# Gathering a scan's partial-array products into four stretches of matmuls

## The chip, the cores and the metric

The kernel runs on one core of one Trainium2 chip. The metric is the device time of one execution in microseconds; for the kernel before it is 1631.19 us, the median of three runs (1631.13 to 1631.39). A core has a matmul engine (TensorE, PE), whose weight loads are shown apart (PEld), a vector engine (VectorE, DVE), an engine for activation functions (ScalarE, ACT), a general one (GpSimd, POOL), a queue for transfers (SyncE, SP), and 16 DMA engines. PE writes its results into banks of PSUM, and a bank must be read by another engine before it is written again.

## The reference, cut to what matters

The kernel computes one step of a decoder of two layers, for 1024 prompt tokens and 8 x 8 sample tokens (1088 columns in all): first a state-space layer (SSD), then a pooling layer. The change lies in the state-space layer's scan, which takes chunks of 128 tokens, for eight groups of four heads with 64 rows each:

```python
def ssd_scan(x, dt, A, B, C, h0):
    ...
    CB = jnp.einsum('bctgn,bcsgn->bctsg', C, B)
    xdt = x * dt[..., None]
    y_intra = jnp.einsum('bctsgr,bcsgrp->bctgrp', CB[..., None] * decay, xdt)
    decay_end = jnp.exp(acum[:, :, -1:] - acum)
    chunk_states = jnp.einsum('bctgn,bctgr,bctgrp->bcgrpn', B, decay_end, xdt)
    chunk_decay = jnp.exp(acum[:, :, -1])
    def step(h, inp):
        s, d = inp
        return d[..., None, None] * h + s, h
    h_final, h_prev = lax.scan(step, ...)
    y_inter = jnp.einsum('bctgn,bctgr,bcgrpn->bctgrp', C, jnp.exp(acum), h_prev)
    y = (y_intra + y_inter).reshape(b, L, H, P)
    return y, h_final.reshape(b, H, P, N)
```

Then y is gated with z, divided by its root mean square over a group's 256 rows, and multiplied by the output weights:

```python
    gated = (y * jax.nn.silu(z.astype(jnp.float32))).reshape(b, L, N_GROUPS, D_INNER // N_GROUPS)
    gated = gated * lax.rsqrt(jnp.mean(gated * gated, axis=-1, keepdims=True) + EPS)
    ...
    return gated.astype(h.dtype) @ w_out, new_conv, new_ssm
```

The sample tokens start from eight states h0 of their own. Each layer's input is shifted, scaled and gated by vectors that come from the conditioning (adaLN): `mod = sc @ ada_w[i] + ada_b[i]`. All is float32.

## The kernel before, in words

Tokens lie along the free axis, features on the 128 partitions. A weight matrix is split into a high and a low part, and every product of the projections is three matmuls of a 128 x 128 block with 360 or 364 tokens (`mm1`, L182 to L184). These use the whole array.

**Scans and fills.** `ssd_layer` runs eight scans, g = 0 to 7, one after the other. Each is a Python generator (`scan_group`); between its steps, `FILL[g]` says how many units of other work are put in from the generator `self.fill` (`beside`). A unit is 24 full matmuls, a third of a projection tile or a piece of the output projection. In scans 0 to 4 the units are the projections of the groups 1, 2, 3, 4 and 6 (`BESIDE`), in scans 5 to 7 the first parts of the output projection, whose inputs were stored to DRAM (`gyd`) and are loaded and split again (`gr` to `gh` and `gl`, L742, L743).

**One scan.** `front(c)` prepares chunk c: B·C (L545) and three transposes (L549) into a bank `tr`; on ACT the exponentials ea (L543), M (four relus L556, one exponential L557), the copy Bt (L566) and cd (L574); on DVE cb, M, xd and ea (L559 to L575). Chunks go in pairs. `states(c)` makes the pair's state sums S (L588, full array) and two additions of h on DVE (L593 for the first of all, L597), with a multiplication by the decay on POOL between (L596). `rows(c)` makes the pair's output y: for each chunk and head, M·xd (L609) and, where there is a state, ea·h (L613). These use 64 of the array's columns, two heads side by side in two column halves; DVE adds the result to y (L580). The sample tokens need Z (L628, 32 columns), zsc on DVE, and four pairs of products (L641 and L644, 64 columns), and their front uses `dup` (L437, 64 columns) for the transposes; `state_sample` updates the sample's states (L660 to L665).

**The tail of a scan** runs into the next one, as the generator `rest`. It gates y (L700 to L702), squares it, and sums the squares with ones in 32 columns (L708); ACT then loads its table (L301) and takes logarithm and exponential (L711, L309); the result goes to DRAM and comes back as a broadcast rs (L713, L716), DVE multiplies y by it (L720), and y is stored to `gyd`.

**adaLN.** The vectors of the second layer and the gates of both are 16 blocks. Each is 8 sums of 32 columns into a bank (L253: 16 records with four heads, `ada_block`), a copy mp on ACT (L258), and two small full matmuls that pick the tokens (L262). Fourteen of the blocks are put into the projections of `BESIDE`, after the second and third units of the tiles 1, 2 and 3 (`ada_plan`); two come late.

**What sets the order.** A scheduler gives each engine its order, once, when the kernel is built: program order is the priority, and an instruction goes ahead of another when what it needs is there earlier by the scheduler's own estimate. `high_priority`, `issue_after` and dependencies added by hand steer it. In the kernel before, the row products, dup, Z, the sums of adaLN and those of squares stand each where the program issues them, with projection matmuls between them where the scheduler found them ready.

Of the kernel before, what the change touches and what calls it, by code (L numbers as in the profile page):

```python
# [50 lines left out]
FILL = (((1,) * 10 + (2,),) * 4 + ((1,) * 9 + (4, 5),) + ((3, 2, 2, 2, 2, 2, 2, 2, 2, 2, 3),) * 2 + ((2, 2, 2, 1, 1, 1, 1, 1, 2, 2, 1),))  # L51
# [46 lines left out]
class Build:  # L98
# [81 lines left out]
    def mm1(self, ps, w, k, act, ch, first, last):  # L180
        nc, (hi, lo), (ah, al), (a, n) = self.nc, w, act, ch
        nc.tensor.matmul(ps[:, :n], hi[:, k, :], ah[:, a:a + n], start=first, stop=False)  # L182
        nc.tensor.matmul(ps[:, :n], hi[:, k, :], al[:, a:a + n], start=False, stop=False)  # L183
        nc.tensor.matmul(ps[:, :n], lo[:, k, :], ah[:, a:a + n], start=False, stop=last)  # L184
# [55 lines left out]
    def ada_block(self, src):  # L240

# [56 lines left out]

    def ln_set(self, mm=None):

        ins = self.nc.scalar.preload_act_table_set("natural_log_exp_and_others")  # L301
        if mm is None:
            self.tc.keep_in_program_order(ins)
        else:
            self.tc.add_manual_dep(ins.ins, mm.ins.name, mybir.DependencyInfo(mybir.DependencyClass.Sync, mybir.DependencyReason.DATA), reason="ln_set")
# [81 lines left out]
    def proj_group(self, G):  # L387

        for ii in range(4):
# [17 lines left out]
            ada = self.ada_do(self.ada_plan[G["g"], ii]) if (G["g"], ii) in self.ada_plan else iter(())  # L407
            for c in range(3):
# [3 lines left out]
                if c:  # L412
                    next(ada, None)
# [90 lines left out]
    def scan_group(self, g, T):  # L504
# [16 lines left out]
        h = [None]  # L521
# [12 lines left out]
        def front(c):  # L534
# [9 lines left out]
            pt = pp.tile([P, 512], F32, tag="tr", bufs=2, name=self.name("tr"))  # L544
            nc.tensor.matmul(pt[:L, 384:384 + L], B[:, tok], C[:, tok], start=True, stop=True)  # L545
            for i, t in enumerate((xs[0], xs[1], B)):
                o = pt[:, 128 * i:128 * i + 128]
                if c < 8:
                    nc.tensor.transpose(o, t[:, tok], self.ident)  # L549
                else:  # L550
                    self.dup(o, t[:, tok])
# [31 lines left out]
        def states(c, F):  # L583
# [5 lines left out]
            for i in range(2):  # L589
                cd, Si = F[i][5], S[:, 256 * i:256 * i + 256]  # L590
                hn = gp.tile([P, 4, 64], F32, tag="h", bufs=3, name=self.name("h"))
                if h[-1] is None:
                    nc.vector.tensor_copy(hn.rearrange("p r q -> p (r q)"), Si)  # L593
                else:
                    hd = gp.tile([P, 4, 64], F32, tag="hd", bufs=1, name=self.name("hd"))
                    nc.gpsimd.tensor_tensor(out=hd, in0=h[-1], in1=cd.unsqueeze(2).to_broadcast([P, 4, 64]), op=ALU.mult)  # L596
                    nc.vector.tensor_tensor(out=hn, in0=hd, in1=Si.rearrange("p (r q) -> p r q", r=4), op=ALU.add)  # L597
                h.append(hn)

        def rows(c, F):  # L600

            py = [pp.tile([P, 512], F32, tag="y", bufs=2, name=self.name("y")) for _ in range(2)]
            for i in range(2):
                tok, M, xdt, _, _, _, ct = F[i]
                hc, a = h[-3 + i], 128 * i
                for q in range(2):
                    for rr in range(2):
                        r, o = 2 * q + rr, slice(64 * rr, 64 * rr + 64)
                        nc.tensor.matmul(py[q][o, a:a + 128], xdt[:, r, :], M[:, r, :], start=True, stop=(hc is None))  # L609
                    if hc is not None:  # L610
                        for rr in range(2):
                            r, o = 2 * q + rr, slice(64 * rr, 64 * rr + 64)
                            nc.tensor.matmul(py[q][o, a:a + 128], hc[:, r, :], ct[:, r, :], start=False, stop=True)  # L613
            for q in range(2):
                evac_y(py[q], q, slice(128 * c, 128 * c + 256), 256)

        def sample_inter():

# [4 lines left out]
            nc.gpsimd.tensor_copy(mv[:, :, 1, 8:16], cv[:, :, 1, :])  # L623
            Z = pp.tile([P, 512], F32, tag="S", bufs=1, name=self.name("Z"))
# [5 lines left out]
            zsc = gp.tile([P, 4, 64], F32, tag="hd", bufs=1, name=self.name("zsc"))  # L630
# [4 lines left out]
        def back_sample(F, zsc):  # L635
            tok, M, xdt, xde, Bt, _, ea = F
            for q in range(2):
                py = pp.tile([P, 512], F32, tag="y", bufs=2, name=self.name("y"))
                for rr in range(2):
                    r, o = 2 * q + rr, slice(64 * rr, 64 * rr + 64)  # L640
                    nc.tensor.matmul(py[o, :64], xdt[:64, r, :], M[:64, r, :64], start=True, stop=False)  # L641
                for rr in range(2):
                    r, o = 2 * q + rr, slice(64 * rr, 64 * rr + 64)
                    nc.tensor.matmul(py[o, :64], zsc[:, r, :], self.kc[:, K_SEL64:K_SEL64 + 64], start=False, stop=True)  # L644
                evac_y(py, q, tok, 64)
# [46 lines left out]
        F, h = F[0], h[-1]  # L692
        nc.sync.dma_start(self.io["hpT"][g], h.rearrange("p r q -> p (r q)"))
        st = back_sample(F, zsc)
# [9 lines left out]
        state_sample(*st, 1)  # L704

        ps = self.pp.tile([P, 512], F32, tag="y", bufs=2, name=self.name("ms"))
        for j in range(4):
            mm = nc.tensor.matmul(ps[32 * j:32 * j + 32, :272], self.ones[:, :32], sq[0][:, 272 * j:272 * j + 272], start=True, stop=True, tile_position=(0, 32 * j))  # L708
        rs = sq[1][:, :272]
# [526 lines left out]
    def run(self):  # L1236
# [3 lines left out]
        places = [(g, ii) for g in BESIDE for ii in (1, 2, 3) if (g, ii) != (BESIDE[-1], 3)]  # L1240
# [5 lines left out]
        for g in BESIDE:  # L1246
            for ii in range(4):
                items.append((io["win"][6 * g + ii], 8))
                if (g, ii) in self.ada_plan:
# [557 lines left out]
```

## Time and profile before

| what | value |
|---|---|
| median of three runs | 1631.19 us (1631.13 to 1631.39) |
| the profiled execution's own time | 1633.98 us |
| its span, first to last instruction | 1632.2 us |
| mean granted clock of TensorE | 0.994 |
| the eight scans in the trace | about 359 to 1010 us |
| DVE, ACT, POOL busy over the span | 79%, 50%, 30% |
| DMA | 275.60 MB, 169 GB/s in the mean |

The page of the profile is of one execution; engines are named as above. A row of a group names the line, the engine, the operation, "out<-in" by the program's tile names, how often it ran, its busy time and mean ns, and the idle time of the engine just before it with what ended that. A row of the timeline has start, duration, engine, line, operation and shape, and in brackets a wait with its releaser. `128*64` is the part of the array a matmul uses, rows by columns; `128x256` is the size of its input. Ends of matmuls are modelled, so durations of PE rows overlap: the distance between starts is what a matmul took.

### The profile page before, as it was taken

What the parts mean: (1) busy time and instruction counts of PE and PEld (TensorE: products, weight loads), DVE (VectorE), ACT (ScalarE), POOL (GpSimd) and SP (SyncE); (2) the same over time, 40 slices, a digit from 0 to 9 for tenths busy, and PEclk for the clock granted to TensorE, in tenths of its full rate; (3) what the DMA queues carried; (4) which work ended last, traced back from release to release, by engine and by line L of the source; (5) the groups of instructions that cost most, each with busy time, mean ns of one, the idle gap of its engine ahead of it and who ended that gap; (6) DMA issues with size and microseconds to landing.
All of it is one profiled execution on the core that took longest, in us unless ns stands there. A gap on an engine that the chain in (4) does not pass through costs nothing.

```text
span 1632.2 us, 30956 instructions
## 1 busy us (share of the span) xinstructions
PE 1601.1 (98%) x12061; PEld 1524.7 (93%) x12061; DVE 1290.3 (79%) x2140; ACT 816.7 (50%) x1565; POOL 495.2 (30%) x527
## 2 busy tenths in 40 slices
PE   8999999999999999999999999999999999999997
PEld 6899999998899888988998899999999999999997
DVE  6875779777788888789887867988889867577876
ACT  6653334456776767575645536632322333333364
POOL 0233556511221202121212222366667640000241
PEclk9999999999999999999999999999999999999999
DMA  9422232264555554668898533043333369565783
GB/s 346 163 98 84 93 109 71 105 203 133 183 162 167 165 186 135 217 232 299 276 332 284 201 137 111 29 142 112 102 112 99 129 213 367 166 170 173 167 164 119
DMA packets 122306, 275.60 MB, mean 169 GB/s; under 512 B 18192, under 2 KB 59312, under 8 KB 122160
## 3 DMA queue, kind: packets, MB, share of 16 engines
q1 hardware_dynamic: 118128, 260.91, 46.8%
q0 software_dynamic: 4032, 12.72, 4.5%
q8 instruction: 95, 1.56, 0.4%
q14 instruction: 51, 0.42, 0.1%
HBM read 201.12 MB, written 70.23 MB: 166 GB/s over the span
## 4 chain that ended last, share of the span: by engine, by line
PE 82%; DVE 7%; DMA 5%; issue 3%; ACT 2%; POOL 1%; SPq 0%; DVEq 0%; ACTq 0%; POOLq 0%
PE st L982 11%; PE st L980 11%; PE st L981 11%; PE mm L182 10%; PE mm L184 10%; PE mm L183 10%; DMA acb<-acd 2%; PE op L1197 2%; PE op L1198 2%; PE op L1196 2%; PE y L609 2%; PE S L588 2%; PE y L613 2%; PE am L253 1%; PE tr L549 1%
## 5 line engine op out<-in xcount | busy, mean ns | idle before, releaser
L982 PE MATMUL st<-hh,w 128*128 128x272 f32 x832 | 240.8, 289 | 2.3 <-DVE w L176 2.3
L980 PE MATMUL st<-hh,w 128*128 128x272 f32 x832 | 240.2, 289 | 0.0
L981 PE MATMUL st<-hl,w 128*128 128x272 f32 x832 | 239.7, 288 | 0.0
L982 PE MATMUL st<-t,w 128*128 128x272 f32 x624 | 179.6, 288 | 0.0
L980 PE MATMUL st<-t,w 128*128 128x272 f32 x624 | 179.6, 288 | 0.0
L981 PE MATMUL st<-t,w 128*128 128x272 f32 x624 | 179.2, 287 | 0.0
L182 PE MATMUL mm<-hh,wh 128*128 128x364 f32 (+1 forms) x528 | 178.4, 338 | 0.1
L184 PE MATMUL mm<-hh,wl 128*128 128x364 f32 (+1 forms) x528 | 174.6, 331 | 0.0
L183 PE MATMUL mm<-hl,wh 128*128 128x364 f32 (+1 forms) x528 | 173.7, 329 | 0.0
L174 ACT ACTIVATE w<-wr 128x512 fp32r<-128x512 f32 x104 | 65.6, 631 | 190.4 <-PE st L982 156.8
L982 PEld LDWEIGHTS st<-hh,w 128*128 128x128 f32 x832 | 156.4, 188 | 3.4 <-DVE w L176 3.4
L980 PEld LDWEIGHTS st<-hh,w 128*128 128x128 f32 x832 | 156.7, 188 | 0.3 <-issue 0.3
L981 PEld LDWEIGHTS st<-hl,w 128*128 128x128 f32 x832 | 156.8, 188 | 0.0
L596 POOL TENSOR_TENSOR hd<-h,cd 128x256 f32<-128x256 f32 x56 | 47.1, 842 | 353.6 <-DVE h L597 195.4
L182 PE MATMUL mm<-gh,wh 128*128 128x364 f32 (+1 forms) x384 | 130.2, 340 | 2.1 <-ACT raw L419 2.1
L1197 PE MATMUL op<-b,w 128*128 128x272 f32 x448 | 129.0, 288 | 1.3 <-DVE b L1126 1.3
L1198 PE MATMUL op<-b,w 128*128 128x272 f32 x448 | 129.0, 288 | 0.7 <-DVE w L1170 0.7
L1196 PE MATMUL op<-b,w 128*128 128x272 f32 x448 | 129.6, 289 | 0.0
L184 PE MATMUL mm<-gh,wl 128*128 128x364 f32 (+1 forms) x384 | 127.1, 331 | 0.0
L183 PE MATMUL mm<-gl,wh 128*128 128x364 f32 (+1 forms) x384 | 126.7, 330 | 0.1
L980 PEld LDWEIGHTS st<-t,w 128*128 128x128 f32 x624 | 117.7, 189 | 0.0
L982 PEld LDWEIGHTS st<-t,w 128*128 128x128 f32 x624 | 117.3, 188 | 0.0
(293 smaller groups left out, 4613.7 us busy)
## 6 DMA issues: line engine op xcount, KB each, us to landing
wr<-win SPq DMA_DIRECT2D x48, 512.0 KB, 3.7
acb<-acd SPq DMA_DIRECT2D x64, 256.0 KB, 3.9
wr<-pin SPq DMA_DIRECT2D x32, 512.0 KB, 3.6
wr<-pout SPq DMA_DIRECT2D x28, 512.0 KB, 3.9
x<-x1d SPq DMA_DIRECT2D x24, 544.0 KB, 6.3
x1d<-x SPq DMA_DIRECT2D x22, 544.0 KB, 5.4
wr<-pout POOLq DMA_DIRECT2D x20, 512.0 KB, 5.5
x<-xT SPq DMA_DIRECT2D x16, 544.0 KB, 6.0
```

The costliest lines, as they stand in the source:

```text
L174: self.nc.scalar.activation(hi, src, AF.Copy)
L182: nc.tensor.matmul(ps[:, :n], hi[:, k, :], ah[:, a:a + n], start=first, stop=False)
L183: nc.tensor.matmul(ps[:, :n], hi[:, k, :], al[:, a:a + n], start=False, stop=False)
L184: nc.tensor.matmul(ps[:, :n], lo[:, k, :], ah[:, a:a + n], start=False, stop=last)
L588: nc.tensor.matmul(S[:, 256 * i:256 * i + 256], Bt, xde.rearrange("p r q -> p (r q)"), start=True, stop=True)
L596: nc.gpsimd.tensor_tensor(out=hd, in0=h[-1], in1=cd.unsqueeze(2).to_broadcast([P, 4, 64]), op=ALU.mult)
L980: nc.tensor.matmul(ps[c][:, :QUART], hi[:, k], xh[:, t], start=(k == 0), stop=False)
L981: nc.tensor.matmul(ps[c][:, :QUART], hi[:, k], xl[:, t], start=False, stop=False)
L982: nc.tensor.matmul(ps[c][:, :QUART], lo[:, k], xh[:, t], start=False, stop=(k == 3))
L1196: nc.tensor.matmul(ps[:, :QUART], hi[:, k], xh, start=k == 0, stop=False)
L1197: nc.tensor.matmul(ps[:, :QUART], hi[:, k], xl, start=False, stop=False)
L1198: nc.tensor.matmul(ps[:, :QUART], lo[:, k], xh, start=False, stop=k == 7)
```

## The change

What was issued one after the other in `rows`, `back_sample`, `sample_inter`, the tail and `ada_block` is issued as one stretch for each pair of chunks, in a function `visit(c, F, F8, zsc)` for c = 0, 2, 4 and 6:

- All row products of the pair, inside `high_priority(HIGH)`. The first of them has an added dependency on the last of the two additions of h of the pair (`behind(mm, hins[-1])`).
- After the last of them (`issue_after`): at c = 0 the sums of the previous scan's squares (`next(rest)`); at c = 4 the sample's B·C, its dups and Z; at c = 6 the sample's four pairs of products, both halves in one bank with the tag S; and at c = 0, 2 and 6 of the scans 0 to 4 the sums of one adaLN block (`ADA`). These are 15 places in place of 14, so that one block comes late in place of two.
- The second step of an adaLN block follows with the next `states` call or at the end of the scan.
- `front(8)`, the loads of h0 and the copies for Z come earlier, B and C are freed with front(8); zsc moves from the tag hd to xl, the squares' sum from y to S.
- `rest` gets two more steps, and is resumed at steps 0, 3 and 5 of the next scan and in visit 0.
- From scan 1 on, the first units of a scan's `FILL` come ahead of its front(0), which is issued after their last matmul. In scans 1 to 4 these are three units, and none comes between front(0), front(1) and the first states.

```diff
-FILL = (((1,) * 10 + (2,),) * 4 + ((1,) * 9 + (4, 5),) + ((3, 2, 2, 2, 2, 2, 2, 2, 2, 2, 3),) * 2 + ((2, 2, 2, 1, 1, 1, 1, 1, 2, 2, 1),))
+FILL = ((1,) * 10 + (2,),) + (((3, 0, 0) + (1,) * 7 + (2,),) * 3 + ((3, 0, 0) + (1,) * 6 + (4, 5),) + ((3, 2, 2, 2, 2, 2, 2, 2, 2, 2, 3),) * 2 + ((2, 2, 2, 1, 1, 1, 1, 1, 2, 2, 1),))
+ADA = (0, 2, 6)
+HIGH = 400
...
+    def behind(self, ins, other):
+
+        self.tc.add_manual_dep(ins.ins, other.ins.name, mybir.DependencyInfo(mybir.DependencyClass.Sync, mybir.DependencyReason.DATA), reason="behind")
...
-            ada = self.ada_do(self.ada_plan[G["g"], ii]) if (G["g"], ii) in self.ada_plan else iter(())
             for c in range(3):
                 ps = self.mm_tile()
                 self.mm3(ps, w, self.hn, CH[c])
                 self.proj_evict(G, ii, raw, ps, c)
-                if c:
-                    next(ada, None)
                 yield
...
-        def rows(c, F):
+        def visit(c, F, F8=None, zsc=None):
...
             py = [pp.tile([P, 512], F32, tag="y", bufs=2, name=self.name("y")) for _ in range(2)]
...
+            with self.tc.high_priority(HIGH):
+                mm = None
...
+                            m = nc.tensor.matmul(py[q][o, a:a + 128], xdt[:, r, :], M[:, r, :], start=True, stop=(hc is None))
+                            if mm is None:
+                                mm = m
+                                self.behind(mm, hins[-1])
...
+                with self.tc.issue_after(m.ins):
+                    if c == 0:
+                        next(rest, None)
+                    if c == 4:
+                        self.pts = pp.tile([P, 512], F32, tag="tr", bufs=2, name=self.name("tr"))
+                        for i, t in enumerate((xs[0], xs[1], B)):
+                            self.dup(self.pts[:, 128 * i:128 * i + 128], t[:, NP:TOK])
+                        nc.tensor.matmul(self.pts[:64, 384:448], B[:, NP:TOK], C[:, NP:TOK], start=True, stop=True)
+                        Z = sample_products()
+                    if c == 6:
+                        _, M, xdt, _, _, _, _ = F8
+                        py8 = pp.tile([P, 512], F32, tag="S", bufs=1, name=self.name("y"))
...
+                    if (g, c) in self.ada_plan:
+                        self.ada = self.ada_do(self.ada_plan[g, c])
+                        next(self.ada)
             for q in range(2):
                 evac_y(py[q], q, slice(128 * c, 128 * c + 256), 256)
+            return sample_inter(Z) if c == 4 else py8
...
         for c in range(0, 8, 2):
             states(c, F)
-            if c == 6:
+            next(self.ada, None)
+            if c < 6:
+                Fn = [front(c + 2)]
+            if c == 2:
+                load_h0()
+                sample_prep()
+            elif c == 6:
                 load_z()
-            Fn = [front(c + 2)]
-            if c == 6:
-                self.slots.free(B)
-            rows(c, F)
-            F = Fn
-            if c == 6:
-                zsc = sample_inter()
-                self.slots.free(C)
             yield
             if c < 6:
-                F.append(front(c + 3))
+                zsc = visit(c, F)
+                Fn.append(front(c + 3))
+                F = Fn
                 if c == 4:
-                    load_h0()
+                    F8 = front(8)
+                    self.slots.free(B, C)
+            else:
+                py = visit(c, F, F8, zsc)
+            if c < 6:
                 yield
...
         state_sample(*st, 1)
-
-        ps = self.pp.tile([P, 512], F32, tag="y", bufs=2, name=self.name("ms"))
+        yield
+
+        ps = self.pp.tile([P, 512], F32, tag="S", bufs=1, name=self.name("ms"))
         for j in range(4):
             mm = nc.tensor.matmul(ps[32 * j:32 * j + 32, :272], self.ones[:, :32], sq[0][:, 272 * j:272 * j + 272], start=True, stop=True, tile_position=(0, 32 * j))
+        yield
...
-        places = [(g, ii) for g in BESIDE for ii in (1, 2, 3) if (g, ii) != (BESIDE[-1], 3)]
+        places = [(g, c) for g in range(len(BESIDE)) for c in ADA]
...
             for i, n in enumerate(FILL[g]):
-                next(sc)
+                if i or not g:
+                    next(sc)
                 for j in range(n):
                     next(self.fill)
-                    if i in (0, 3) and j == 0:
+                    if i in (0, 3, 5) and j == 0:
                         next(rest, None)
+                if g and not i:
+
+                    with self.tc.issue_after(self.last_mm.ins):
+                        next(sc)
```

More of the change, by code (lines that the diff above doesn't have):

```diff
@@ L183, in mm1 @@
         nc.tensor.matmul(ps[:, :n], hi[:, k, :], al[:, a:a + n], start=False, stop=False)
-        nc.tensor.matmul(ps[:, :n], lo[:, k, :], ah[:, a:a + n], start=False, stop=last)
+        self.last_mm = nc.tensor.matmul(ps[:, :n], lo[:, k, :], ah[:, a:a + n], start=False, stop=last)
     def mm3(self, ps, w, acts, ch):
@@ L304, in ln_set @@
         else:
[L305 removed]
+            self.behind(ins, mm)
         return self.tc.issue_after(ins.ins)
@@ L543, in front @@
             nc.scalar.activation(ea[:, :, :L], acb, AF.Exp)
[L544 to L551, printed above, removed]
+            if c < 8:
+                pt = pp.tile([P, 512], F32, tag="tr", bufs=2, name=self.name("tr"))
+                nc.tensor.matmul(pt[:L, 384:384 + L], B[:, tok], C[:, tok], start=True, stop=True)
+                for i, t in enumerate((xs[0], xs[1], B)):
+                    nc.tensor.transpose(pt[:, 128 * i:128 * i + 128], t[:, tok], self.ident)
+            else:
+                pt = self.pts
             M = gp.tile([P, 4, 128], F32, tag="M", bufs=3, name=self.name("M"))
@@ L633, in sample_inter, with back_sample @@
             return zsc
-        def back_sample(F, zsc):
+        def back_sample(F, py):
             tok, M, xdt, xde, Bt, _, ea = F
             for q in range(2):
[L638 to L645, printed above, removed]
+                evac_y(py[:, 64 * q:64 * q + 64], q, tok, 64)
             for i in range(2):
@@ L1479, in ssd_layer @@
         self.out_unit()
-        next(rest)
+        for _ in range(3):
+            next(rest)
         for _ in range(2):
```

55 lines of the change are left out of this document (35 added, 20 removed).

## The prediction

> **What bounds the kernel now.** I read the page first, then the waits of TensorE inside the scans, a table of one steady stretch, and rows of the timeline.
>
> ```profile
> PE 1601.1 (98%) x12061; PEld 1524.7 (93%) x12061; DVE 1290.3 (79%) x2140; ACT 816.7 (50%) x1565; POOL 495.2 (30%) x527
> ```
>
> TensorE (PE) is busy for 98% of the span. The eight scans take about 650 us of it, from 359 to 1010. The next two fences are the table by stretches for one scan amid them (columns: bounds, length, then busy time of PE, PEld, DVE, ACT and POOL, granted clock, DMA share, GB/s) and the waits of PE between 359 and 1012 (total us, times, longest).
>
> ```profile
> 440.00:515.00 75.00, 75.00 (x586) 67.37 (x585) 61.89 (x94) 51.08 (x117) 13.72 (x27) 1.00 0.51 167
> ```
>
> ```profile
> PE S L588 <- ACT Bt L566: 4.5, 3, 2.3
> PE mm L182 <- ACT raw L419: 2.1, 1, 2.1
> PE y L613 <- DVE h L593: 1.4, 1, 1.4
> ```
>
> PE is busy 75.00 of 75.00 us there at a clock of 1.00, and waits 4.5 + 2.1 + 1.4 = 8.0 us in all eight scans. So what shortens the path is less time per matmul; what lengthens it is any wait that PE is now made to see. But busy is not the same as paid for work: the starts of the records show an extra price around each use of a part of the array. The three fences that follow are rows of TensorE's timeline: start, duration, then the operation with the part of the array it uses (128*64 is half of its columns).
>
> ```profile
> 458.77 0.33 PE L182 MATMUL mm<-hh,wh 128*128 128x364 f32 x1
> 458.94 0.32 PE L183 MATMUL mm<-hl,wh 128*128 128x364 f32 x1
> 459.19 0.66 PE L613 MATMUL y<-ea,h 128*64 128x128 f32 x8
> 459.78 0.43 PE L184 MATMUL mm<-hh,wl 128*128 128x364 f32 x1
> 460.05 0.33 PE L182 MATMUL mm<-hh,wh 128*128 128x364 f32 x1
> ```
>
> ```profile
> 424.05 0.32 PE L184 MATMUL mm<-hh,wl 128*128 128x364 f32 x1
> 424.30 1.07 PE L253 MATMUL am<-wr,scp 128*32 128x256 f32 x16
> 425.30 0.43 PE L182 MATMUL mm<-hh,wh 128*128 128x360 f32 x1
> 425.57 0.33 PE L183 MATMUL mm<-hl,wh 128*128 128x360 f32 x1
> ```
>
> ```profile
> 558.83 0.48 PE L609 MATMUL y<-M,xd 128*64 128x128 f32 x4
> 559.05 0.48 PE L613 MATMUL y<-ea,h 128*64 128x128 f32 x4
> 559.46 0.42 PE L628 MATMUL Z<-h,ctm 128*32 128x256 f32 x4
> ```
>
> Full-size matmuls follow each other at 0.17 us (458.77 to 458.94). Four 64-column records take 0.22 (558.83 to 559.05, from one group to another that uses the same two column halves), so eight cost 0.44.
>
> **The price of one excursion.** From 458.94 to 460.05 are 1.11 us. Work alone would be 0.17 + 0.44 + 0.17 = 0.78. The excursion to 64 columns and back therefore costs 0.33 (0.34 with the unrounded starts, which I take). With 32 columns the two edges show alike: 0.25 instead of 0.17 on the way in, 0.27 for the first full matmul after it. A direct step from 64 to 32 columns takes 0.41 (559.05 to 559.46) instead of 0.22 for four records of its kind: 0.2, and no more.
>
> **What the change removes and adds.** In the order of PE's instructions I counted, for scans 0 to 7, the entries from the full array into 64 or 32 columns, and the steps between these two. Before: 82 entries (58 + 24) and 9 steps. Changed: 34 entries (32 + 2) and 26 steps. One excursion per chunk pair holds the row products of both chunks, with the adaLN sums, the previous scan's squares or the sample's products appended. The number of matmuls differs by one. So
>
> 48 × 0.34 = 16.3 us gained, 17 × 0.2 = 3.4 us paid: −12.9 us.
>
> The Trainium skill ("TensorEngine Tiling (Array Packing)", Tiling Modes, Key Properties) says that changing the tiling mode, not merely the tile, drains TensorE. The trace agrees: 0.34 for leaving and coming back, and nothing between column halves of one size (0.22 for every four). By that rule each step between 64 and 32 columns is a switch like any other, half an excursion; 173 switches become 94, and 79 × 0.17 = 13.4 us would be gained, 0.5 more than my sum.
>
> **The new wait for the second state.** In the kernel before, the first products of a pair need only M and xd; they hide the time until the state h is there. Now the first product of each visit waits for the last h addition of its pair. Rows of TensorE, of VectorE, and of TensorE again:
>
> ```profile
> 480.36 1.13 PE L588 MATMUL S<-xd,Bt 128*128 128x256 f32 x4
> ```
>
> ```profile
> 481.60 0.42 DVE L597 TENSOR_TENSOR h<-hd,S 128x256 f32<-128x256 f32 x1 [0.70 <-PE S L588]
> 482.75 0.42 DVE L597 TENSOR_TENSOR h<-hd,S 128x256 f32<-128x256 f32 x1 [0.73 <-POOL hd L596]
> ```
>
> ```profile
> 377.81 1.03 PE L588 MATMUL S<-xd,Bt 128*128 128x256 f32 x4
> 378.68 0.38 PE L545 MATMUL tr<-xbc,xbc 128*128 128x128 f32 x2
> 378.90 0.49 PE L549 MATMUL tr<-kc,xbc 128*128 128x128 f32 x3
> 379.32 0.33 PE L609 MATMUL y<-M,xd 128*64 128x128 f32 x2
> ```
>
> From the end of S (480.36 + 1.13 = 481.49) to the second h (482.75 + 0.42 = 483.17) are 1.68 us with DVE free. In the changed order, visit c=2 of six scans (1 to 4, 6, 7) has the least in between: B·C and three transposes (377.81 + 1.03 = 378.84 to 379.32: 0.48) and six full matmuls (6 × 0.166 = 1.0), 1.48 in all. That leaves 0.2, rounded up to 0.3 for the semaphores: six times, +1.8 us. All other visits have at least 1.9 us of work there, at most of them 2.5 and more, and I take nothing; if DVE is busy with a 1.2 to 1.4 us instruction at that moment, each costs up to that. What is queued behind the waiting matmul is all of PE's work, so every bit of this wait is paid; the lower end, no wait, is 0, the upper end is the second rival.
>
> **adaLN's second step.** The selection (L262) needs mp, which ScalarE copies from the sums. Before, a projection unit of at least 24 matmuls (4 us) stood between them. Now, in visit c=0 of scans 1 to 4, only the transposes (0.48) and six matmuls (1.0) do. From the visit's start PE needs for its 12 products 0.7, for the squares and the sums 0.3 and 1.0 (the row at 424.30), for the steps between sizes 0.5, then these 1.5, and some 0.5 for the starts between the kinds: I estimate 4.5 to L262. On ACT's side the next fence gives, for the groups of ACT in the scans, count, busy time and mean (ns) of one instruction.
>
> ```profile
> L556 ACT ACTIVATE M<-acb,tka 128x128 f32<-128x128 f32 (+1 forms) x288 | 93.1, 384 | 39.3 <-PE y L609 38.7 <-DMA acb<-acd 0.6
> L557 ACT ACTIVATE M<-M 128x512 f32<-128x512 f32 (+1 forms) x72 | 43.1, 599 | 0.3
> L543 ACT ACTIVATE ea<-acb 128x512 f32<-128x512 f32 (+1 forms) x72 | 42.9, 596 | 13.0 <-DMA acb<-acd 12.3 <-PE y L613 0.2
> ...
> L301 ACT ACT_TABLE_LOAD x9 | 11.5, 1283 | 8.2 <-PE ms L708 8.1
> ...
> L258 ACT ACTIVATE mp<-am 128x256 f32<-128x256 f32 x16 | 6.0, 377 | 4.3 <-PE am L253 4.1
> ```
>
> Four relus (1.3; pipelined, somewhat less than 4 × 0.384), ea 0.60, the exponential of M 0.60, the table load 1.28 and mp 0.38 make 4.1, and the first relu must wait until the visit's first products have read the M before it, which I put at 0.7: 4.8 against 4.5, 0.3 × 4 = +1.2 us. Ends: 0, if ACT is ahead, and 4 × 1.3 = 5.2, if a table load's time more is lost. In visits c=2 and c=6 there are about 1.8 and 0.7 us of matmuls between the sums and L262, against mp's 0.38; I take nothing there.
>
> **The boundary between output parts.** TensorE's and ScalarE's timelines around 730:
>
> ```profile
> 729.62 0.32 PE L184 MATMUL mm<-hh,wl 128*128 128x360 f32 x1
> 732.00 0.43 PE L182 MATMUL mm<-gh,wh 128*128 128x364 f32 x1 [2.06 <-ACT raw L419]
> ```
>
> ```profile
> 729.80 1.11 ACT L742 ACTIVATE gh<-gr 128x1088 fp32r<-128x1088 f32 x1 [0.88 <-DMA gr<-gyd]
> ...
> 732.72 1.11 ACT L701 ACTIVATE z<-xbc 128x1088 f32<-128x1088 f32 x1
> ```
>
> PE waited 2.06 us for the eviction that frees a bank, because ACT stood at gh, which had waited for a load. In the changed order two gate instructions of 1.11 (partly overlapped) stand ahead of that eviction instead of behind it, 1.35 later, and PE arrives about 0.9 later because of its new order: +0.4. Ends: −2.1 (the wait goes) and +3 (the gyd store, now two units later, delays the load as well).
>
> **Costed at nothing.** The earlier front(8), the earlier h0 load and the freeing of B and C move work by one visit, on POOL (13.72 busy of 75) and SP, with slots that were free. zsc in the tag xl and ms in the tag S must be read before the tag's next user; each has a unit of 24 matmuls (4.0 us) or more in between, against a table load of 1.28 and one Ln. If that cover went, S would hold up states by about a microsecond in seven scans. The previous scan's tail is resumed later; nothing but the boundary above reads its result soon.
>
> **The sum.** −12.9 + 1.8 + 1.2 + 0.4 = −9.5 us. The profiled execution took 1633.98, 2.79 above the median of the runs, 1631.19; so it would take 1624.5, and the median 1621.7.
>
> **The rivals.** *First, slower: DVE late for the state.* The previous scan's two last multiplications (L720) now stand, in DVE's order of scans 1 to 7, ahead of the additions of h for which visit c=4 waits, and they wait for a broadcast load. What the view of the tile rs says of that load (idle time of DVE for it, and us to landing):
>
> ```profile
>   DMA rs<-rsd: 2.4, 1
> ...
> DMA to landing us min/median/max: 3.9/5.1/7.5
> ```
>
> The load landed 3.9 to 7.5 us after issue, and DVE once waited 2.4 us for it. I estimate about 1 us of slack at a median load. The place decides the case once each of the seven later scans loses (9.5 + 3.3) / 7 = 1.8 us there. At 2.4 each, 16.8 us are lost: 1621.7 + 16.8 = 1638.5. Against it: seven out of eight loads before were waited for by nobody on DVE.
>
> *Second, same: every visit waits a little.* DVE has 61.89 busy of 75, so a free DVE, as in 480.36, is the kinder case. At 0.4 us for each of the 32 visits, 12.8 instead of 1.8, the time is 1621.7 + 11.0 = 1632.7, hardly other than before. For it: before, the state often arrived only 0.4 to 0.6 us ahead of its first reader, which stood behind four products that now wait too. Against it: the scheduler has placed at least 1.9 us of matmuls in most gaps.
>
> *Third, faster still: the old waits go too.* If the 8.0 us of waits in this stage vanish, because Bt has longer to be ready, the time is 1621.7 − 8.0 = 1613.7. For it: 4.5 of them are for Bt, which a scan that starts with three units in a row gives more time. Against it: the chain of loads at the boundary remains, and scan 0 begins as before. That the change leaves the switches as they are is excluded by the count.
>
> **How the numbers follow.** I take 0.2% (3.3 us) as what can be told from no change. Forecast as summed, with the bounds of its terms: 0.69; third rival: 0.10; second: 0.10; first: 0.11. Faster: 0.79, same: 0.10, slower: 0.11. The range goes from 1615 (with no new wait at all 1631.19 − 12.9 = 1618.3, and 3.3 of the third rival's 8.0) to 1631 (the upper ends, +5.2 at adaLN and +3 at the boundary, and most of the second rival). Left out are the first rival and the far ends, together about 2 in 10.
>
> **What would show it.** In the changed profile: the 64-column rows come in one run of 16 for a pair and are followed directly by 32-column rows; PE's busy time in the scans falls by about 13 us; a wait "y <- DVE h" of about 0.2 to 0.3 us appears six times, and one "am <- ACT mp" four times. Wrong would be: waits of y for h in all visits (second rival), a wait of DVE for rs followed by PE's wait for h in scans 1 to 7 (first), or a full matmul after the long stretch that takes longer than the 0.27 us it takes after a short one.

## The result, and the profile after

The changed kernel takes 1646.06 us (median of four runs, 1644.66 to 1647.38) against 1631.29 us of the kernel before on the same chip: a ratio of 1.0087, with an interval of 1.0069 to 1.0104. It is 14.8 us slower, where 9.5 us faster was forecast. The profiled execution took 1644.85 us, its span is 1643.1 us.

The page after, with the line of busy times and the one of the chain that ended last (the work that set the span, followed back from its end, by engine):

```profile
PE 1595.7 (97%) x12061; PEld 1525.0 (93%) x12061; DVE 1294.1 (79%) x2140; ACT 812.2 (49%) x1564; POOL 510.2 (31%) x527
...
PE 71%; DVE 12%; DMA 7%; issue 5%; ACT 3%; POOL 2%; SPq 0%; DVEq 0%; ACTq 0%; POOLq 0%
```

The chain before was:

```profile
PE 82%; DVE 7%; DMA 5%; issue 3%; ACT 2%; POOL 1%; SPq 0%; DVEq 0%; ACTq 0%; POOLq 0%
```

PE is busy for 5.4 us less (1601.1 before), and yet the span is 10.9 us longer: PE now stands idle for 47 us instead of 31. PE's share of the chain has fallen from 82% to 71%, and DVE's has risen from 7% to 12%. The waits of PE in the scans, between 359 and 1025 (total us, times, longest):

```profile
PE y L618 <- DVE h L601: 13.3, 15, 2.0
PE S L592 <- ACT Bt L570: 5.2, 7, 1.6
PE S L697 <- ACT xs L694: 1.8, 1, 1.8
PE mm L184 <- DVE gs L808: 1.6, 1, 1.6
```

8.0 us of waits have become some 23, and 13.3 of them are the new wait: the first row product (L618) for h (L601).

**Where the time went.** The same matmuls stand between the 289th and the 2737th product of `mm1` in both kernels, so this stretch can be compared directly; it holds the eight scans but for the last tail. From the starts of all its PE records I took three parts: what each use of a part of the array costs beyond its matmuls (with its waits taken out), what clocks below 1.00 cost, and all else beyond the same 577.0 us of work, which I count as waits.

| kernel | stretch | switching | half clock | waits |
|---|---|---|---|---|
| before | 623.9 | 34.6 | 3.4 | 8.9 |
| changed | 634.4 | 20.6 | 3.4 | 33.4 |

Switching costs 14.0 us less, somewhat more than forecast. Waits cost 24.5 us more. y's for h are 15.2 us now and were 1.5, and most of the rest stands at places that the comparison with the prediction's steps goes through; some 4 us I did not place. That is the whole result: +10.5 in this stretch of the profiled execution. (By the starts a wait is longer than in the view, where it counts from the modelled end of the product before it.)

The price of leaving the full array is as before, as these rows of PE's timeline of the changed kernel show (a visit c=0 without a wait):

```profile
614.76 0.33 PE L184 MATMUL mm<-hh,wh 128*128 128x360 f32 x1
614.93 0.33 PE L185 MATMUL mm<-hl,wh 128*128 128x360 f32 x1
615.18 0.88 PE L618 MATMUL y<-M,xd 128*64 128x128 f32 x12
615.89 0.39 PE L625 MATMUL y<-ea,h 128*64 128x128 f32 x4
616.11 0.39 PE L618 MATMUL y<-M,xd 128*64 128x128 f32 x4
616.33 0.39 PE L625 MATMUL y<-ea,h 128*64 128x128 f32 x4
616.65 0.67 PE L748 MATMUL ms<-z,ones 128*32 128x272 f32 x8
617.13 1.05 PE L256 MATMUL am<-wr,scp 128*32 128x256 f32 x16
```

The way in takes 0.25 instead of 0.17 (614.93 to 615.18), as it did before. The step from 64 to 32 columns takes 0.32 (616.33 to 616.65) instead of 0.22: 0.1, where the forecast had 0.2. From squares to sums, both on 32 columns, nothing is added.

**Why h is late.** Three fences show visit c=6 of scan 1: VectorE, GpSimd and TensorE.

```profile
485.96 0.69 DVE L566 TENSOR_TENSOR xd<-tr,tkx 128x512 f32<-128x512 f32 x1
486.56 1.63 DVE L564 TENSOR_TENSOR M<-M,cb 128x512 f32<-128x512 f32 x1
488.11 2.43 DVE L579 TENSOR_TENSOR ea<-xbc,ea 128x512 f32<-128x512 f32 x1
490.46 0.21 DVE L563 TENSOR_TENSOR cb<-tr,kc 64x64 f32<-64x64 f32 x1
490.59 0.67 DVE L566 TENSOR_TENSOR xd<-tr,tkx 128x512 f32<-128x512 f32 x1
491.19 0.41 DVE L564 TENSOR_TENSOR M<-M,cb 64x256 f32<-64x256 f32 x1
491.52 0.40 DVE L601 TENSOR_TENSOR h<-hd,S 128x256 f32<-128x256 f32 x1
...
492.65 0.42 DVE L601 TENSOR_TENSOR h<-hd,S 128x256 f32<-128x256 f32 x1 [0.53 <-POOL hd L600]
```

```profile
485.70 4.29 POOL L681 TENSOR_TENSOR h<-h,ea 128x1024 f32<-128x1024 f32 x2
492.00 0.61 POOL L600 TENSOR_TENSOR hd<-h,cd 128x256 f32<-128x256 f32 x1 [2.02 <-DVE h L601]
```

```profile
490.84 0.33 PE L186 MATMUL mm<-hh,wl 128*128 128x364 f32 x1
493.13 0.44 PE L618 MATMUL y<-M,xd 128*64 128x128 f32 x4 [1.96 <-DVE h L601]
```

PE waits 2.0 us until the second addition of h ends at 493.07. This addition is late because DVE is: M takes 1.63 us and ea 2.43, where the same instructions take 0.68 elsewhere. Both run while POOL multiplies the sample's state h0 by its decay (L681, two instructions, 4.29 us). xd beside them, which reads one of its inputs from a PSUM bank, keeps its 0.69. And by the records of the trace POOL's two instructions end at 487.63 and 489.99, while M ends at 488.19 and ea at 490.54: each ends some 0.55 us after one of POOL's, as if it had waited for that end and had then run at about its own speed.

The Trainium skill ("SBUF — State Buffer", Who interferes with whom) says: VectorE and GpSimd share a pair of ports; a VectorE instruction with two inputs in SBUF contends with a GpSimd instruction that reads SBUF; and the shared pair is an exclusive lock. The trace agrees: M and ea have both inputs in SBUF and end some 0.55 us after a POOL instruction does, xd has one in PSUM and is not slowed.

In the source of the kernel before, the decay stands behind the sample's row products. There it ran at 485.29, after both additions of that pair (481.60 and 482.75), and hit another ea, for which nothing waited:

```profile
485.29 4.52 POOL L647 TENSOR_TENSOR h<-h,ea 128x1024 f32<-128x1024 f32 x2 [0.26 <-issue]
```

```profile
486.03 1.98 DVE L575 TENSOR_TENSOR ea<-xbc,ea 128x512 f32<-128x512 f32 x1
```

In the source of the changed kernel the decay is as late as before, in `back_sample`. But it needs only h0 and front(8)'s exponential, and both now come a visit earlier. So the scheduler put it as early as it could, ahead of the last pair's additions.

### The profile page after: what moved, and what is told of

Its sections match the earlier page's. It is cut to its first block, busy times and chain, and to the rows that moved or that the text cites. A ratio compares the mean times of both kernels' runs of the same rounds, so it can differ in the third digit from the quotient of the medians.

```text
span 1643.1 us, 30946 instructions
## 1 busy us (share of the span) xinstructions
PE 1595.7 (97%) x12061; PEld 1525.0 (93%) x12061; DVE 1294.1 (79%) x2140; ACT 812.2 (49%) x1564; POOL 510.2 (31%) x527
## 4 chain that ended last, share of the span: by engine, by line
PE 71%; DVE 12%; DMA 7%; issue 5%; ACT 3%; POOL 2%; SPq 0%; DVEq 0%; ACTq 0%; POOLq 0%
PE st L1023 11%; PE st L1021 11%; PE st L1022 11%; PE mm L184 8%; PE mm L185 8%; PE mm L186 8%; PE op L1238 2%; PE op L1239 2%; PE op L1237 2%; DMA wr<-win 2%; PE y L618 1%; PE am L256 1%; DVE M L564 1%; DMA acb<-acd 1%; DVE xbc L356 1%
## 5 line engine op out<-in xcount | busy, mean ns | idle before, releaser
L600 POOL TENSOR_TENSOR hd<-h,cd 128x256 f32<-128x256 f32 x56 | 52.6, 939 | 274.1 <-DVE h L601 134.3
```

## The experiments

Three theories for the waits of y for h: **P**, the early decay on POOL stretches DVE's work; **F**, front(8)'s own work on DVE stands ahead of the additions; **D**, the added dependency itself is what costs. All times below are medians beside runs of the kernel before on the same chip, and the ratio, with its interval, is to that. Those runs of the kernel before have medians between 1629.15 and 1631.66 us, so two kernels are compared by their ratios where it matters. Where two intervals overlap, a difference between the two kernels is not shown; the changed kernel's is 1.0069 to 1.0104.

### e1: hold the decay

```diff
-                nc.gpsimd.tensor_tensor(out=h0[i], in0=h0[i], ..., op=ALU.mult)
+                self.behind(nc.gpsimd.tensor_tensor(out=h0[i], in0=h0[i], ..., op=ALU.mult), hins[-1])
```

> Edit: the two multiplications of h0 by the sample's decay on POOL wait for the last addition of h of the scan; nothing else moves on PE. Theory P (these multiplications run beside DVE ahead of the last pair's additions and stretch DVE's M and ea from 0.68 to 1.6 and 2.4 us, so that h is late): the waits of y for h in visit c=6, 2.0 us in each of scans 0 to 4 and 1.3 and 0.65 in two later ones, fall to 0.3 or less; 8 to 10 us less in all, about 1637. Theory F (front(8)'s own work on DVE, 1.3 to 1.5 us ahead of the additions, is what makes h late): the waits stay at 1.3 or more, at most 4 us less, 1642. Theory D (the added dependency alone makes the waits): no change, 1646.

Measured: 1634.25 us, ratio 1.0018 (1.0008 to 1.0028), 11.8 us less than the changed kernel. The same visit, VectorE and TensorE:

```profile
480.99 0.68 DVE L564 TENSOR_TENSOR M<-M,cb 128x512 f32<-128x512 f32 x1
481.59 0.68 DVE L579 TENSOR_TENSOR ea<-xbc,ea 128x512 f32<-128x512 f32 x1
482.19 0.21 DVE L563 TENSOR_TENSOR cb<-tr,kc 64x64 f32<-64x64 f32 x1
482.33 0.67 DVE L566 TENSOR_TENSOR xd<-tr,tkx 128x512 f32<-128x512 f32 x1
482.93 0.41 DVE L564 TENSOR_TENSOR M<-M,cb 64x256 f32<-64x256 f32 x1
483.26 0.41 DVE L601 TENSOR_TENSOR h<-hd,S 128x256 f32<-128x256 f32 x1
...
484.46 0.42 DVE L601 TENSOR_TENSOR h<-hd,S 128x256 f32<-128x256 f32 x1 [0.59 <-POOL hd L600]
```

```profile
485.27 0.33 PE L186 MATMUL mm<-hh,wl 128*128 128x364 f32 x1
485.52 0.44 PE L618 MATMUL y<-M,xd 128*64 128x128 f32 x4
```

M and ea are back at 0.68, front(8)'s instructions still stand ahead of the additions, and the wait is gone (0.25 from 485.27 to 485.52 is the way in). P is shown for the scans 0 to 4: there the waits at the visits c=6 fall from 9.4 us, by the starts, to 0.2. PE's own order is all but untouched (6 of 4668 records stand elsewhere). F is excluded as their cause, since front(8)'s work stands where it stood. In the scans 5 and 6 the same waits were 2.0 us in sum and are 1.9, so the decay does not explain those. In the compared stretch e1 takes 623.9, as the kernel before: switching 20.6, no half clock, and 26 of waits. Of the 10.5 us that it is shorter than in the changed kernel, 3.4 are half clock. Some 2 us came back as new waits, of state_sample's product for ACT (L697 for xs: 2.2 by the page, 1.8 in the changed kernel) and of the adaLN's second step for mp (1.4).

### e2: without the added dependency

```diff
                                 mm = m
-                                self.behind(mm, hins[-1])
```

> Edit: the added dependency of the first row product on the last addition of h is left out; the order is the scheduler's. Theory D: the waits of y for h go, 10 to 13 us less, about 1634. Theories P and F: the first products start, and PE waits at the first product that needs h, four or twelve records later; each visit gains at most 0.2 to 0.6 us of its wait, at most 5 us in all, about 1642, and possibly nothing, as the scheduler may place the stretch earlier.

Measured: 1666.4 us, ratio 1.0217 (1.0202 to 1.0233). D fails in the form in which it was tested, that the time would fall without the dependency, and so does my expectation under P and F: it is 20 us slower than with the dependency. Without it the scheduler no longer keeps a visit in one piece: it issues the products in groups of eight as they become ready. The compared stretch has 110 uses of a part of the array instead of 34 and takes 657.3 us. PE's waits there:

```profile
PE y L618 <- DVE xbc L584: 9.3, 6, 2.9
PE tr L551 <- ACT Bt L570: 2.7, 2, 1.4
PE y L618 <- DVE M L564: 2.1, 3, 1.1
```

The waits for h are gone, and waits for the eviction of y's banks have come. The dependency is what holds the stretches together. That it costs nothing is not shown by this; e9 and e10 take that up.

### e3: front(8) later

```diff
             elif c == 6:
+                F8 = front(8)
+                self.slots.free(B, C)
                 load_z()
...
-                if c == 4:
-                    F8 = front(8)
-                    self.slots.free(B, C)
```

> Edit: front(8) is issued after the states of the last pair instead of right after visit c=4. Theory F: its 1.3 to 1.5 us on DVE now stand behind the additions, 6 us less, about 1640. Theory P: the decay on POOL needs front(8)'s exponential, which is now later, so the multiplications fall behind the additions too: 8 to 10 us less, about 1637, unless visit c=6 now waits for the sample's M, which would show as a wait of y (the sample's product) for DVE M. Theory D: no change, 1646.

Measured: 1642.24 us, ratio 1.0064 (1.0047 to 1.0081), 3.8 us less by the medians, with overlapping intervals. The compared stretch is 0.9 us shorter (633.5), so where a gain would come from is not shown. The waits at c=6 stayed (y for h: 15.9 us in all). This run does not test F as was meant: most of front(8)'s work on DVE now stands behind the first addition, but still ahead of the second, for which the visit waits. F rests on e1. P's expectation failed too, for a reason that the rows give. ACT made front(8)'s exponential early all the same, so POOL ran the decay where it had, and M and ea were stretched as before:

```profile
481.85 4.29 POOL L681 TENSOR_TENSOR h<-h,ea 128x1024 f32<-128x1024 f32 x2
```

```profile
482.71 1.62 DVE L564 TENSOR_TENSOR M<-M,cb 128x512 f32<-128x512 f32 x1
484.26 2.43 DVE L579 TENSOR_TENSOR ea<-xbc,ea 128x512 f32<-128x512 f32 x1
...
486.74 0.40 DVE L601 TENSOR_TENSOR h<-hd,S 128x256 f32<-128x256 f32 x1
487.27 0.84 DVE L564 TENSOR_TENSOR M<-M,cb 64x256 f32<-64x256 f32 x1
488.03 0.67 DVE L566 TENSOR_TENSOR xd<-tr,tkx 128x512 f32<-128x512 f32 x1
488.63 0.40 DVE L601 TENSOR_TENSOR h<-hd,S 128x256 f32<-128x256 f32 x1
```

### e4: the old FILL

```diff
-FILL = ((1,) * 10 + (2,),) + (((3, 0, 0) + (1,) * 7 + (2,),) * 3 + ...)
+FILL = (((1,) * 10 + (2,),) * 4 + ((1,) * 9 + (4, 5),) + ...)
```

> Edit: FILL as in the kernel before, one unit between the fronts and the first states instead of three ahead of them. All theories: the waits in visit c=6 stay. If the three units in a row cost (waits of the first states for Bt of 0.25 to 0.4 us in scans 1 to 4): 1 to 2 us less, 1644.5. If they were what kept other waits away: 2 us or more longer, 1648 and up.

Measured: 1648.18 us, ratio 1.0103 (1.0088 to 1.0118), 2.1 us more by the medians, with overlapping intervals. The three units in a row are not the cause; without them the waits of y for h are 21.0 us instead of 13.3.

### e5 and e8: the additions of h first

```diff
+            with self.tc.high_priority(HIGH):
-            for i in range(2):
+                for i in range(2):
                     cd, Si = F[i][5], S[:, 256 * i:256 * i + 256]
...
```

e5 is e1 with this, e8 the changed kernel with this alone.

> Edit: e1, and the multiplications and additions of h get the same high priority as the row products, so that DVE and POOL take them ahead of other work. Theory Q (what is left of the waits of y for h, 5.3 us, comes from other DVE work that stands ahead of the additions, above all in scans 5 to 7): these waits fall to 1 or 2 us, and the time to about 1630. Theory R (they come from the chain S, h, POOL, h itself, 1.7 us): no change against e1, 1634.

> Edit: the priority of e5 alone, with POOL's multiplications of h0 where the changed kernel has them. It separates the two things that make h late in visit c=6: the order on DVE (front(8)'s 1.3 us ahead of the additions) and the stretch of M and ea beside POOL (2.7 us). Stretch alone decides: visits c=6 of scans 0 to 4 still wait 1.3 us or more each, about 1641 to 1643. Order alone decides: their waits fall under 0.5 us, about 1636.

Measured: e5 1639.8 us, ratio 1.0052 (1.0036 to 1.0068), 5.5 us more than e1; e8 1648.77 us, ratio 1.0117 (1.0094 to 1.0139), 2.7 us more than the changed kernel, with intervals that overlap. Both are misses. In e8 the waits at c=6 of scans 1 to 4 did fall away, and the time did not. POOL's decay came nearly two microseconds earlier still (483.95), and hit what stands there. A DVE instruction on 64 columns took 1.97 us (0.22 elsewhere), and ACT waited for POOL to be done with the ea that it wanted to overwrite:

```profile
484.21 1.97 DVE L369 SCALAR_TENSOR_TENSOR xbc<-raw,raw 128x64 f32<-128x64 f32 x1
```

```profile
488.02 0.63 ACT L548 ACTIVATE ea<-acb 128x512 f32<-128x512 f32 x1 [2.75 <-POOL h L681]
```

In this scan PE then waited at the states 0.64 us for zsc, behind that DVE instruction, and 0.52 for Bt, which stands behind that ea on ACT. So the early decay still costs, with another victim. That is not all: transposes wait 3.7 us for Bt in all scans (0.3 in the changed kernel), and in this scan that wait ends at 483.25, ahead of the decay. Such waits come with the priority itself. In e5, where the decay is held, transposes wait 5.2 us for Bt as well, and y still 7.2 for h. I take it that what the additions overtook now comes later; beyond this, why e5 is slower than e1 stays open.

### e6 and e7: the adaLN sums by themselves

e6 is e1 with the sums a unit after the visit, and the second step another unit later; e7 is e5 and e6 together.

```diff
             with self.tc.issue_after(m.ins):
...
-                        next(self.ada)
+                        self.sp = True; next(self.ada); self.sp = False
...
-            states(c, F)
-            next(self.ada, None)
-            ...
-            yield
+            next(self.ada, None); states(c, F)
+            ...
+            yield; next(self.ada, None)
```

(With `sp` set, the block only takes its weights at the visit, and yields once more ahead of its matmuls.)

> Edit: e1, and the sums of the adaLN blocks are taken out of the stretches: a unit later, as excursions of their own, with the second step another unit later. By the price of a switch 15 more excursions at 0.33 and 15 fewer steps from 64 to 32 columns at 0.13: +3.0 us; the waits of the second step for mp (1.4 us) and those of 0.2 us at four places go: -2.2. Together about 1 us more than e1, 1635. If gathering the sums is worth nothing, 2 us less, 1632; if a switch costs twice as much as I read it, 1638.

> Edit: e5 and e6 together. If the parts add up: e1 plus the difference that each of the two made, about 1631; below the kernel before (1631) by no more than 2 us.

Measured: e6 1638.07 us, ratio 1.0052 (1.0032 to 1.0072), between 1633.7 and 1641.8; e7 1639.46 us, ratio 1.0057 (1.0036 to 1.0079). In the compared stretch of its profiled execution, the fastest of its seven, e6 takes 626.1, 2.2 more than e1, where about 1 was forecast; the median is 3.8 more, past the end of my range. By the starts e6 has 16 uses of a part of the array more than e1, and only 3 steps between 64 and 32 columns fewer, where 15 fewer were forecast. So gathering the sums is worth something; how much of the 3.8 is their price is not shown. e7 misses its expectation of 1631, and it is not the sum of what e5 and e6 lost either (which would be 1643.6).

### e9 and e10: wait for the first addition only

While reading e1 I saw what the forecast had passed over: a pair's own products read the state before the pair and the state after its first chunk (`h[-3 + i]`). The second addition, for which they now wait, is read only by the next pair.

```diff
-                                self.behind(mm, hins[-1])
+                                self.behind(mm, hins[-2])
```

e9 is the changed kernel with this, e10 is e1 with this.

> Edit: the first row product waits for the first of the pair's two additions of h instead of the second. The pair's own products read the state before the pair and the state after its first chunk; the second addition is read only by the next pair. From the first addition to the end of the second are 1.2 us (481.60 to 482.75 before). Theory Q2 (the dependency waits for more than the data need): each wait in visit c=6 falls by up to 1.2 us, 2.0 to 0.9, the small ones vanish, 6 to 8 us less, about 1639. Rival (the scheduler only moves the stretches earlier by as much, since it sees the wait gone): no change, 1646.

> Edit: e1 and e9 together. Theory Q2: the 5.3 us of waits of y for h that e1 has left fall to 1 or less; 4 to 5 us less than e1, about 1630, at or just below the kernel before. Rival (stretches move earlier): as e1, 1634.

Measured: e9 1643.02 us, ratio 1.0082 (1.0052 to 1.0113), 3.0 us less by the medians, but hardly less by the ratios, and a miss against 1639; e10 1628.48 us, ratio 0.9987 (0.9973 to 1.0002), 5.8 us less than e1 by the medians and 5.1 by the ratios. In e9 the waits of y for h fall from 13.3 to 2.8, as Q2 said. But the gain is lost: with the visit out of the way, the decay makes states wait, at three places for 3.2 us each by the starts. These rows show the first, on ACT and PE:

```profile
487.59 0.63 ACT L548 ACTIVATE ea<-acb 128x512 f32<-128x512 f32 x1 [3.83 <-POOL h L681]
```

```profile
488.80 1.22 PE L592 MATMUL S<-xd,Bt 128*128 128x256 f32 x2 [3.16 <-ACT Bt L570]
```

With the decay held, these waits are gone. The longest waits of PE in e10's scans:

```profile
PE y L618 <- DVE h L601: 1.3, 1, 1.3
PE mm L184 <- DVE gs L808: 1.2, 1, 1.2
PE y L618 <- DVE h L597: 1.1, 1, 1.1
PE S L592 <- ACT Bt L570: 1.1, 2, 0.8
```

Its compared stretch takes 615.0 us, 9.0 less than before (3.4 of it the half clock).

### e11 and e12: one step more, and e10 again

e11 moves the adaLN's second step after visit c=6 one unit down:

```diff
-        next(self.ada, None)
         h = h[-1]
...
         st = back_sample(F8, py)
         yield
+        next(self.ada, None)
```

> Edit: e10, and after visit c=6 the second step of the adaLN block comes one unit later. In e1 that step waited for mp 1.4 us by the page, 1.9 by the starts, at three places. If that is all it does: 1.5 to 2 us less than e10, about 1628. If ACT's order, which moves with it, makes new waits for Bt: no gain.

> The kernel of e10 once more, with more rounds, since its interval of 0.9973 to 1.0002 leaves open whether the gathering, with both mended, is a gain. By the scans' own time (614.95 against 623.92 us, of which 3.4 are half-clock stretches that only the profiled run of the kernel before shows there): 5 to 6 us less than before in the mean, ratio 0.9965. If the half-clock stretches that fall into some runs eat that up: 0.999 or more.

Measured: e11 1635.67 us, ratio 1.0028 (1.0007 to 1.0049), a miss: 7 us more than e10 (its interval overlaps that of e12, the same kernel as e10), with waits of S for Bt of 6.3 us, and 10.2 us of half clock in the scans of its profiled execution. e12, the kernel of e10: 1632.2 us, ratio 1.0001 (0.9990 to 1.0012), where 0.9965 was expected, or 0.999 and more if half clock ate up the gain. So with both mends the gathering is worth nothing that can be measured; e10's 0.9987 was the better end. The profiled execution of e10 was the shortest of its ten, that of e12 the longest of its twelve: e12's is 10 us longer, and its compared stretch takes 624.3, no less than before. The two part at one place above all, 4 us at 858 in scan 6:

```profile
861.47 1.11 ACT L783 ACTIVATE gh<-gr 128x1088 fp32r<-128x1088 f32 x1 [2.75 <-DMA gr<-gyd]
862.48 0.26 ACT L570 ACTIVATE Bt<-tr 128x128 f32<-128x128 f32 x1
```

ACT stood for 2.75 us at gh, for a load of what the last scan stored, with Bt behind it, and PE waited for Bt. That load took 10.3 us from issue to landing here, and 8.6 in e10's execution, where ACT did not wait for it. Which of the other waits take up the saved switches in e12 is not worked out.

## Why the prediction was wrong, by its own steps

- **What bounds the kernel; the price and the count of switches**: right. The gain was 14.0 us by the starts, where −12.9 was forecast. The mis-sized term is the step from 64 to 32 columns: 0.1, not 0.2. With 0.1 the prediction's own sum gives 48 × 0.34 − 17 × 0.1 = 14.6. Its other reading, in which such a step is half an excursion (0.17) by the rule of the Trainium skill ("TensorEngine Tiling (Array Packing)", Tiling Modes, Key Properties), does not fit the measured 0.1 either.
- **The new wait for the second state, +1.8**: right for the place that it named, wrong in its reach. The six visits c=2 waited 0.27, 0.25, 0.24, 0.24, 0.32 and 0.34 us by the starts, 1.7 together. The sentence "All other visits have at least 1.9 us of work there ... and I take nothing" is one of the two that failed: the visits c=6 waited 11.4 us. Its condition was named (DVE busy at that moment), and not followed up for the visit whose DVE and POOL work the change had moved. It also took for given that the second addition must be waited for; the data need only the first. That costs some 3 to 5 us of e1's time (ratio 1.0018, against 0.9987 in e10 and 1.0001 in e12).
- **Costed at nothing: front(8), h0 and the copies "move work by one visit, on POOL (13.72 busy of 75)"**: this is the step that lost the forecast: put at nothing, it cost 9.2 us of waits at the visits c=6 of scans 0 to 4, which e1 takes away. A mean load of 18% says nothing on what 4.3 us of POOL do at one place. What moved was not only what the source moved: the decay, left where it was in the source, became ready earlier, and the scheduler took it forward. It should have been looked for in POOL's new order, and priced by the row of the kernel before that shows it beside a stretched ea (1.98 instead of 0.68).
- **adaLN's second step, +1.2**: measured four times 0.2, 0.8 us in sum; right.
- **The boundary between parts, +0.4 with an end of +3**: PE waits there 1.9, 0.7 and 1.8 us (at 738, 747 and 759) where it waited 2.2 before: +2.2, within the range. But the wait that the term was about, for the eviction of raw, fell to 0.7; the other two are for other operations (xs on ACT, gs on DVE), so that the sum fits is in part luck.
- **Not seen at all**: the waits of states for Bt rose from 5.0 to 8.4 us by the starts; the third rival had counted on their going.
- **The rivals**: the first had the mechanism in its general form, DVE late for the state that the visit waits for, and nearly the price (16.8 us; 13.3 measured by the page). But it had the wrong work on DVE and the wrong visit: L761 stood ahead of visit c=4, and there the waits were 0.15 us in four scans. DVE waited for rs once, 2.2 us. The second rival, 0.4 us at each of 32 visits, would have been 12.8; that the sum came near is luck, for the spread did not: 11.4 of 15.2 us lay at seven visits. 0.11 for slower was too little for a change that puts all of PE's queue behind a chain over three engines.

## What to carry to other kernels

A wait in front of the bounding engine turns every delay of the chain behind it into time, so the chain's engines have to be looked at where it runs, by instruction, and not by their mean load. Where a scheduler decides the order, moving an operation earlier also moves what depends on it: compare each engine's order, and hold what is not urgent. And make a stretch wait for the last thing that it reads, no later one: here a wait for one state too many cost 3 to 5 us, from e1 to e12 and e10, which are one kernel (the interval of e12 just overlaps that of e1).

## What the runs showed of the hardware that was not expected

Two instructions of POOL of 1.9 and 2.4 us stretched DVE instructions with both inputs in SBUF by up to 1.75 us (0.68 to 2.43), and one on 64 columns from 0.22 to 1.97, while those with an input in PSUM kept their time.

A wait of PE of 2 us was sometimes followed, about 1 us later, by 7 us at half clock. In the changed kernel four such waits of 1.9 to 2.0 us stand at the same place of scans 1 to 4, and only the one at 568 was followed by it, in a window with these numbers (columns as in the prediction; the clock is the third from the end):

```profile
571.00:578.00 7.00, 7.00 (x64) 4.93 (x61) 3.45 (x5) 3.36 (x9) 0.85 (x3) 0.52 0.42 135
```

Such a stretch costs about half its length. In the compared stretch of the profiled executions the clock cost nothing in e1 and e10, 1.7 us in e12 (the same kernel as e10), 3.4 in the kernel before and the changed one, 8.5 in e9 and 10.2 in e11; so a few us between single executions can be the clock alone. The Trainium skill ("TensorE: Matmul & The Clock Gate", Part 1: The HAM clock gate) describes a free-running window of about 3.4 us and a drop to half the clock after an idle one. The lengths seen here, 3.4 and 7 us, agree with such a window, and that the same wait has it in one scan and not in the next agrees with its running free; but a wait of 2 us, shorter than such a window, was enough here.
